# Down weight sums added by DMA, the last up tile and the first Down units in one order, own PSUM banks for the chains, another order of the gate stage

## The chip, the cores and the metric

The kernel runs on one core of a Trainium2 chip. The metric is the time of one execution on the device in microseconds. The kernel before took 2066.22 us (median of three runs, 2062.82 to 2066.92).

## The reference

One layer of a streaming encoder on 1056 tokens (1024 of a prompt, 32 of a sample; width 1024), all in float32:

```
z = rms(x) @ w_in            -> GLA q,k,v,r,gate | band q,k,v | merge gates gA,gB
mix = (sigmoid(gA)*(oa @ w_br_a) + sigmoid(gB)*(ob @ w_br_b)) @ w_out;   x += rms(mix)
a, g = split(rms(x) @ w_up)  (2 x 2816 columns)
y = (gelu(conv3(g)) * a) @ w_down;                                       x += rms(y)
gate = sigmoid(rms(x) @ w_ple_gate);                                     x += rms(gate * (p @ w_ple))
```

`oa` is a gated linear recurrence over four heads, `ob` a softmax attention over a band of chunks. Outputs are y, the keys and values, the recurrence states and the convolution state.

## The kernel before

Tokens lie along the free dimension, features along the 128 partitions. Every product is made of three TensorE products of halves (high x high, high x low, low x high), so each weight tile and each operand is split: ScalarE (ACT) copies to a rounded high part (`whi`, `mh`, `u`), VectorE (DVE) subtracts to get the low part (`wlo`, `ml`). SP issues the loads, POOL (GpSimd) issues most stores and the loads of Down's operands; each of these engines works through its own instructions in order.

The stages follow one another: w_in (52 projections, `project`, with the recurrence and the attention between), w_br_b, w_br_a, w_out, four up tiles as plain products (`up_plain`, `up_one`), 18 up tiles f = 4 to 21 by a Strassen-like scheme with seven products of quarter size (`up_strassen`, 24 matmuls of 264 columns each), Down (`down_unit`) and the gate stage.

The Strassen products read sums t1 to t4 of quarters of the normalised x, made from pairs of loads into the two `hn` buffers (`quarter_sums`, `quarter_third`, `quarter_last`); t4 is written over a part of `mh`/`ml` that the plain tiles read. `activate` (L1050) finishes an up tile: convolution, gelu, product, store to DRAM (`d_b`). After each odd tile `sums` makes four sums of the tile pair's rows, in `hn` buffers, one behind each product of the tiles that follow, and stores them too.

Down is such a scheme again: seven products q by four output pairs j, 28 units of 66 matmuls. Its row operands ("entries", two rows of 128 each) are loaded from `d_b` into `uraw` and split into nine `u` tiles; its weights are four sums of w_down's tiles, `d_s`, made in SBUF during w_br_a (`weight_sums`: 24 loads, 48 DVE operations, 24 stores). `chain(j)` gives a unit its PSUM banks: three sets "two" in turn, and "aux" for j = 3, which the sums of the norms (`sum_mm`) use too. `at(u, ...)` puts the norm's steps behind unit u: r1 (norm of the first half of y), `n_join` (residual added), r2 (norm for the gate), `n_oper` (operands); `MID` puts the norm's sums inside a unit. `presplit` splits w_ple_gate into `d_g` in units 2 to 16.

The gate stage goes through 24 tiles (8 "one" of 48 matmuls, then 16 of 24); `on(g, ...)` puts work behind tile g: `g_sig1` and `g_pair` (sigmoid), `g_mult` (product, square, sum of squares), the norm f1 of the first half, f3, and `final`, which adds into y by an accumulating DMA.

PE, DVE and ACT follow the written order in w_br_b to the plain up tiles and from Down on (`manual_schedule`); elsewhere a scheduler orders them by its own estimate. SP and POOL are ordered by the scheduler throughout.

## Time and profile before

| | |
|---|---|
| three runs | 2062.82, 2066.22, 2066.92 us |
| profiled execution | 2066.53 us, span 2064.5 us, mean granted TensorE clock 0.972 |
| TensorE, VectorE, ScalarE, GpSimd busy | 95%, 62%, 46%, 21% of the span |

A window of the trace gives, for each engine, the time it was busy and its instructions; the clock is the share of full speed granted to TensorE. A line of the waits reads: engine, tile and line that waited, what released it, microseconds in total, times, and the longest. In a timeline a row has its start, its duration, engine, line, operation, out<-in, and in brackets the idle time ahead of it and what ended that. Places in the trace, in microseconds of the span: w_in up to 900, w_br_b and w_br_a to 1070, w_out to 1170, plain up tiles to 1280, Strassen up tiles to 1680, Down to 1932, gate stage to the end.

### The profile page before, as it was taken

How to read it: one execution, taken by the hardware profiler on the slowest of the kernel's cores; microseconds unless marked ns; L12 is line 12 of the kernel's file. 1: busy time of each engine (PE TensorE's matmuls, PEld its weight loads, DVE VectorE, ACT ScalarE, POOL GpSimd, SP SyncE). 2: the span in 40 equal slices, each digit the busy share in tenths (PEclk: the TensorE clock that was granted, in tenths of full speed). 3: DMA queues.
4: the chain of work that ended last, by engine and by line, in shares of the span. 5: the costliest groups of instructions: out<-in, count | busy, mean ns of one | idle time of the engine just before them, and what ended most of it. 6: DMA issues, size and time to landing. Idle time of an engine off the chain costs nothing. (4 is left out here: it accounts for less than half of the span.)

```text
span 2064.5 us, 34547 instructions
## 1 busy us (share of the span) xinstructions
PE 1953.1 (95%) x13584; PEld 1908.2 (92%) x13584; DVE 1288.8 (62%) x2538; ACT 941.6 (46%) x1691; POOL 426.6 (21%) x489
## 2 busy tenths in 40 slices
PE   8999999999999999989998999799999979997985
PEld 7999999999999999989997999699999979997985
DVE  7556655465465663765763776677777764566565
ACT  6455556364553744643223554243334344454444
POOL 4422322321121211112320111011111121124102
PEclk9999999999999999999999999899999979998997
DMA  7212212211321212277984455523222358875667
GB/s 271 65 54 81 70 45 75 61 63 53 98 73 60 91 53 93 78 218 251 358 303 142 145 169 187 172 89 120 89 94 89 110 179 292 294 240 192 195 202 151
DMA packets 107534, 292.30 MB, mean 142 GB/s; under 512 B 12260, under 2 KB 36780, under 8 KB 107372
## 3 DMA queue, kind: packets, MB, share of 16 engines
q1 hardware_dynamic: 85420, 218.12, 32.0%
q0 software_dynamic: 21664, 71.63, 10.3%
q8 instruction: 106, 1.74, 0.3%
q14 instruction: 56, 0.46, 0.1%
q10 hardware_dynamic: 288, 0.36, 0.1%
HBM read 200.21 MB, written 89.85 MB: 141 GB/s over the span
## 5 line engine op out<-in xcount | busy, mean ns | idle before, releaser
L225 PE MATMUL mm<-xh,whi 128*128 128x352 f32 x1248 | 412.0, 330 | 0.0
L227 PE MATMUL mm<-xh,wlo 128*128 128x352 f32 x1248 | 411.8, 330 | 0.0
L226 PE MATMUL mm<-xl,whi 128*128 128x352 f32 x1248 | 409.7, 328 | 0.0
L205 POOL TENSOR_TENSOR wlo<-raw,whi 128x512 fp32r<-128x512 f32 x130 | 181.4, 1399 | 719.4 <-ACT whi L204 666.8
L225 PEld LDWEIGHTS mm<-xh,whi 128*128 128x128 f32 x1248 | 235.3, 189 | 1.6 <-DVE ev L349 0.4
L226 PEld LDWEIGHTS mm<-xl,whi 128*128 128x128 f32 x1248 | 235.0, 188 | 1.7 <-issue 0.3
L227 PEld LDWEIGHTS mm<-xh,wlo 128*128 128x128 f32 x1248 | 234.6, 188 | 1.1
L1395 PE MATMUL two<-u,whi 128*128 128x264 f32 x984 | 189.1, 292 | 6.8 <-DVE u L1360 3.8
L1214 PE MATMUL two<-mh,whi 128*128 128x264 f32 x576 | 164.0, 289 | 13.2 <-ACT mh L1151 8.0
L1215 PE MATMUL two<-ml,whi 128*128 128x264 f32 x576 | 165.2, 288 | 3.1 <-DVE ml L1152 3.1
L1395 PEld LDWEIGHTS two<-u,whi 128*128 128x128 f32 x984 | 158.8, 196 | 8.4 <-DVE u L1360 4.6
L1216 PE MATMUL two<-mh,wlo 128*128 128x264 f32 x576 | 164.9, 287 | 0.0
L204 ACT ACTIVATE whi<-raw 128x512 fp32r<-128x512 f32 (+1 forms) x146 | 89.6, 621 | 162.6 <-PE mm L226 99.2
L1395 PE MATMUL two<-u,wlo 128*128 128x264 f32 x492 | 143.5, 292 | 2.0 <-DMA wlo<-d_g 2.0
L1214 PEld LDWEIGHTS two<-mh,whi 128*128 128x128 f32 x576 | 109.2, 191 | 14.9 <-ACT mh L1151 8.9
L1215 PEld LDWEIGHTS two<-ml,whi 128*128 128x128 f32 x576 | 110.3, 191 | 3.9 <-DVE ml L1152 3.9
L1216 PEld LDWEIGHTS two<-mh,wlo 128*128 128x128 f32 x576 | 110.3, 192 | 0.0
L1395 PEld LDWEIGHTS two<-u,wlo 128*128 128x128 f32 x492 | 96.5, 196 | 2.4 <-DMA wlo<-d_g 2.4
L349 DVE TENSOR_TENSOR ev<-mm,rstd 128x352 f32<-128x352 f32 x120 | 61.4, 518 | 55.6 <-PE mm L227 55.0
L1204 ACT ACTIVATE whi<-ws 128x512 fp32r<-128x512 f32 x72 | 45.5, 632 | 103.2 <-PE two L1215 76.9
L1395 PE MATMUL two<-u,dhi 128*128 128x264 f32 x452 | 86.1, 291 | 2.0 <-ACT dhi L1386 2.0
L225 PE MATMUL mm<-mh,ahi 128*128 128x352 f32 x240 | 78.8, 328 | 8.9 <-ACT ahi L880 8.9
(490 smaller groups left out, 5147.8 us busy)
## 6 DMA issues: line engine op xcount, KB each, us to landing
raw<-in_w_in SPq DMA_DIRECT2D x52, 512.0 KB, 3.8
uraw<-d_b POOLq DMA_DIRECT2D x38, 528.0 KB, 5.8
raw<-in_w_up SPq DMA_DIRECT2D x27, 512.0 KB, 3.6
hn<-d_hn SPq DMA_DIRECT2D x24, 528.0 KB, 4.5
draw<-d_s SPq DMA_DIRECT2D x16, 704.0 KB, 4.6
d_b<-hn POOLq DMA_DIRECT2D x20, 528.0 KB, 4.7
d_b<-av POOLq DMA_DIRECT2D x33, 264.0 KB, 2.4
sraw<-in_w_up SPq DMA_DIRECT2D x17, 512.0 KB, 4.0
```

The source lines that it names most:

```text
L204: ac.activation(hi[-1][:, d], raw[:, b], AF.Copy)
L205: eng.tensor_tensor(lo[-1][:, d], raw[:, b], hi[-1][:, d], op=ALU.subtract)
L225: pe.matmul(ps, h, xh(kt), start=(first and i == 0), stop=False)
L226: pe.matmul(ps, h, xl(kt), start=False, stop=False)
L227: pe.matmul(ps, l, xh(kt), start=False, stop=(last and i == n - 1))
L349: return lambda ps, s: ve.tensor_tensor(t[:, s], ps, rstd(s), op=ALU.mult)
L1204: ac.activation(h, x, AF.Copy)
L1214: pe.matmul(ps[:, j, :HC], w[0][:, k], x[0][:, k, s], start=st, stop=False, skip_group_check=True)
L1215: pe.matmul(ps[:, j, :HC], w[0][:, k], x[1][:, k, s], start=False, stop=False, skip_group_check=True)
L1216: pe.matmul(ps[:, j, :HC], w[1][:, k], x[0][:, k, s], start=False, stop=sp_, skip_group_check=True)
L1395: pe.matmul(ps, w, x, start=st, stop=sp_, skip_group_check=True)
```

## The change

Seven edits that hang together:

1. **Down weight sums.** `d_s` is made during w_in by `down_sums`: 16 plain copies from DRAM to DRAM on SP and 16 accumulating DMAs on POOL, one DMA of 704 KB at each of the first 32 projections. Signs are chosen so that only additions are needed; `evac` and the row sums take the other signs.
2. **presplit** goes from Down into the w_br_a loop, on that loop's `ev` tiles.
3. **Order around the plain up tiles.** `quarter_third` comes ahead of the activation of tiles 1 and 2, and no row sums stand ahead of it.
4. **Row sums** no longer use the tiles in SBUF: `activate` stores both halves of each tile, and `row_sums` reads four rows back, makes the four sums and stores each. ROW_JOBS hangs the pairs on tiles 5, 6, 7, 9, 11 and so on; the last pair's go behind units 1 and 2.
5. **Last up tile and first units.** Tile 21 is written in one fixed order with the first four entries' loads (in `hn` buffers) and splits and unit 0's weights (`ahead`); its last quarter is finished behind the splits of entries 4 and 5. Entries live in the rows of `mh`/`ml` (`slots`) and one more tile.
6. **PSUM and norms in Down.** The chains have four named sets; the sum for r1 stands at the start of unit 21, that for r2 in unit 25, and the steps around them are moved; a unit's weights are split ahead of the evacuation of the unit before.
7. **Gate stage.** The sigmoid stands apart from the product (`g_sig`), a square is added when the next comes (`settle`), the products of the first half stand earlier, f1's total at tile 13, and all of f3's `final` behind the last tile.

```diff
+    def down_sums():
+        def step(d, src, j):
+            if src[0] == "sum":
+                x = d_s[src[1], j]
+            else:
+                x = wd[2 * j + src[1], :, src[2]]
+            if d in have:
+                tc.keep_in_program_order(po.dma_start(d_s[d, j], x, accum_op=ALU.add))
+            else:
+                tc.keep_in_program_order(dma.dma_start(d_s[d, j], x))
...
     def project(n, evac):
+        next(sums_left, None)
...
-        for i in range(2 if n in (1, 2, 3, 4) else 1):
-            weight_sums(*parts.pop(0))
-    cp.release()
+        presplit(n)
...
+    def row_sums(i, tile):
+        x, y = tile(), tile()
+        for t, k, d in ((x, 0, B12), (x, 1, B11), (y, 0, B22), (y, 1, B21)):
+            po.dma_start(t[:, k], d[i])
+        yield
+        for o, p, q, op, d in (...):
+            ve.tensor_tensor(o, p, q, op=op)
+            po.dma_start(d[i], o)
+            yield
...
+            if f in ROW_JOBS and muls[0] > 2:
+                next(ROW_JOBS[f], None)
...
-    activate(1, *open_[1, 0])
-    sum_rows(4)
     for f in range(3, UP_PLAIN):
         open_[f, 0] = up_one(f)
     quarter_third()
-    activate(2, *open_[2, 0])
+    for f in range(1, 3):
+        activate(f, *open_[f, 0])
     quarter_last()
...
+    def ahead(m):
+        if m == 3:
+            first_rows()
+        if m < 5:
+            split_entry(m - 3)
+            load_entry(m - 1, hn_tile)
+        elif m == 5:
+            split_entry(2)
+        else:
+            split_weights(0)
+            split_entry(3)
...
     def chain(j):
-        return tl(psum, [P, 2, 512], tag="two" if j < 3 else "aux", bufs=3 if j < 3 else 1)
+        return tl(psum, [P, 2, 512], tag=("c0", "c1", "c2", "aux")[j], bufs=1)
...
-    for i, u in enumerate((22, 22, 23, 23)):
+    for i, u in enumerate((21, 22, 22, 23)):
...
-    at(23, n_total, "r2", "a2")
-    at(24, n_inv, "r2")
+    at(24, n_total, "r2", "a2")
+    at(25, n_inv, "r2")
...
-    MID = {21: lambda: n_sum("r1"), 24: lambda: n_sum("r2")}
+    MID = {21: (0, lambda: n_sum("r1")), 25: (3, lambda: n_sum("r2"))}
...
+    split_entry(4)
+    load_entry(7)
+    split_entry(5)
+    load_entry(8)
+    last_up[2]()
     down_unit(0)
+    split_weights(1)
-    activate(FT - 1, *last_up)
+    activate(FT - 1, *last_up[:2])
...
+        settle(acc)
+        waiting[id(acc)] = i, sq
...
-    on(10, g_one, 0)
-    on(11, g_one, 1)
-    on(12, g_one, 2)
-    on(13, g_one, 3)
-    on(14, n_total, "f1", "g1")
+    on(5, g_one, 0)
+    on(7, g_one, 1)
+    on(11, g_one, 2)
+    on(12, g_one, 3)
+    on(13, n_total, "f1", "g1")
...
-    on(22, final, "f3", 0, three)
-    on(22, final, "f3", 1, three)
...
-    final("f3", 3, three)
+    for i in range(1, 4):
+        final("f3", i, three)
```

How the instructions move on VectorE, at three places. First, behind the last operand sums t1 and t2, while the last plain up tile runs (`gc`: convolution of an up tile, `av`: its product, `hn<-av`: row sums, `xs<-hn` and `t3l`: the operand t3). Before:

```order
L1061 TENSOR_TENSOR av_12365<-gc_12869,av_12365 128x32
L1076 TENSOR_TENSOR hn_12880<-av_12365,hn_12880 128x528
L1076 TENSOR_TENSOR hn_12881<-av_12365,av_12188 128x528
L1076 TENSOR_TENSOR hn_12881<-av_12365,hn_12880 128x528
L1055 SCALAR_TENSOR_TENSOR gc_13103<-gx_12520,vec_69,gc_13103 128x1058
L1205 TENSOR_TENSOR wlo_13182<-raw_13170,whi_13181 128x512
L1056 SCALAR_TENSOR_TENSOR gc_13103<-gx_12520,vec_69,gc_13103 128x1058
L1205 TENSOR_TENSOR wlo_13216<-ws_13212,whi_13215 128x512
L1060 TENSOR_TENSOR av_12521<-gc_13103,av_12521 128x1024
L1061 TENSOR_TENSOR av_12521<-gc_13103,av_12521 128x32
L1055 SCALAR_TENSOR_TENSOR gc_13153<-gx_12888,vec_69,gc_13153 128x1058
L1171 TENSOR_TENSOR xs_13075<-hn_13072,hn_13071 128x528
```

and now:

```order
L1074 SCALAR_TENSOR_TENSOR gc_12765<-gx_12152,vec_69,gc_12765 128x1058
L1075 SCALAR_TENSOR_TENSOR gc_12765<-gx_12152,vec_69,gc_12765 128x1058
L1176 TENSOR_TENSOR xs_13022<-hn_13019,hn_13018 128x528
L1079 TENSOR_TENSOR av_12153<-gc_12765,av_12153 128x1024
L1080 TENSOR_TENSOR av_12153<-gc_12765,av_12153 128x32
L1204 TENSOR_TENSOR ws_13167<-raw_13128 128x512
L1074 SCALAR_TENSOR_TENSOR gc_13050<-gx_12329,vec_69,gc_13050 128x1058
L1204 TENSOR_TENSOR ws_13169<-ws_13167,raw_13127 128x512
L1204 TENSOR_TENSOR ws_13260<-raw_13127,raw_13128 128x512
L1157 TENSOR_TENSOR t3l_13017<-xs_13022,t3h_13016 128x528
L1176 TENSOR_TENSOR xs_13030<-hn_13027,hn_13026 128x528
L1075 SCALAR_TENSOR_TENSOR gc_13050<-gx_12329,vec_69,gc_13050 128x1058
```

The row sums in the `hn` tiles are gone from here, and the first two pairs of t3 stand where the convolution of tile 1 stood.

Second, at the end of the last up tile (`c`, `av`, `gx`: its results, `two`: PSUM, `u<-uraw` before and `ml<-hn` now: the low part of an entry of Down, `wlo<-raw`: unit 0's or the tile's weights). Before:

```order
L1259 TENSOR_TENSOR av_17265<-av_17265,two_17396 128x528
L1387 TENSOR_TENSOR wlo_17529<-raw_17517,whi_17528 128x384
L1262 TENSOR_TENSOR c_2629_17269<-p_2628_17268,two_17395 128x528
L1263 TENSOR_TENSOR gx_17264<-gx_17264,c_2629_17269 128x528
L1232 TENSOR_TENSOR gx_17264<-c_2629_17269,two_17396 128x264
L1233 TENSOR_TENSOR gx_17264<-c_2629_17269,two_17396 128x232
L1234 TENSOR_TENSOR gx_17264<-c_2629_17269,two_17396 128x32
L1360 TENSOR_TENSOR u_17501<-uraw_17507,u_17501 128x2x528
L1360 TENSOR_TENSOR u_17536<-uraw_17509,u_17536 128x2x528
L1360 TENSOR_TENSOR u_17541<-uraw_17511,u_17541 128x2x528
```

and now:

```order
L1356 TENSOR_TENSOR ml_10331<-hn_17298,mh_10330 128x1056
L1212 TENSOR_TENSOR wlo_17451<-ws_17320,whi_17450 128x512
L1356 TENSOR_TENSOR ml_10331<-hn_17300,mh_10330 128x1056
L1204 TENSOR_TENSOR ws_17483<-raw_17302,sraw_17303 128x512
L1212 TENSOR_TENSOR wlo_17486<-ws_17483,whi_17485 128x512
L1267 TENSOR_TENSOR c_2624_17311<-p_2623_17310,two_17327 128x528
L1268 TENSOR_TENSOR av_17307<-av_17307,c_2624_17311 128x528
L1356 TENSOR_TENSOR ml_10331<-hn_17424,mh_10330 128x1056
L1271 TENSOR_TENSOR av_17307<-av_17307,two_17328 128x528
L1366 TENSOR_TENSOR wlo_17543<-raw_17418,whi_17542 128x512
L1366 TENSOR_TENSOR wlo_17547<-raw_17418,whi_17546 128x512
L1366 TENSOR_TENSOR wlo_17551<-raw_17419,whi_17550 128x384
```

The low parts of the entries stand among the tile's last products and results, where they stood behind all of them.

Third, in units 22 to 25 of Down (`z<-z,vec,rs` and `z<-z,pr`: join with the residual, `acc`: squares, `y`: operand of the norm's sum, `z<-z,aux`: evacuation of unit 23). Before:

```order
L1360 TENSOR_TENSOR u_19808<-uraw_19806,u_19808 128x528
L1493 SCALAR_TENSOR_TENSOR z_17648<-z_17648,vec_69,rs_19605 128x528 x2
L1498 TENSOR_TENSOR z_17648<-z_17648,pr_2949_19701 128x2x528
L1452 TENSOR_TENSOR acc_19707<-acc_19707,pr_19817 128x1056
L1493 SCALAR_TENSOR_TENSOR z_17648<-z_17648,vec_69,rs_19605 128x528 x2
L1498 TENSOR_TENSOR z_17648<-z_17648,pr_2965_19811 128x2x528
L1452 TENSOR_TENSOR acc_19707<-acc_19707,pr_19824 128x1056
L1456 TENSOR_TENSOR acc_19707<-acc_19707 128x528
L1459 TENSOR_TENSOR y_2969_19829<-acc_19707,y_2968_19828 128x528
L1435 TENSOR_TENSOR z_17648<-z_17648,aux_19716 128x528
L1437 TENSOR_TENSOR z_17648<-z_17648,aux_19716 128x528
```

and now:

```order
L1356 TENSOR_TENSOR ml_10331<-uraw_19665,mh_10330 128x528
L1541 SCALAR_TENSOR_TENSOR z_17692<-z_17692,vec_69,rs_19564 128x528 x2
L1546 TENSOR_TENSOR z_17692<-z_17692,pr_2896_19667 128x2x528
L1499 TENSOR_TENSOR acc_19579<-acc_19579,pr_19679 128x1056
L1474 TENSOR_TENSOR z_17692<-z_17692,aux_19682 128x528
L1476 TENSOR_TENSOR z_17692<-z_17692,aux_19682 128x528
L1499 TENSOR_TENSOR acc_19579<-acc_19579,pr_19774 128x1056
L1504 TENSOR_TENSOR acc_19579<-acc_19579 128x528
L1507 TENSOR_TENSOR y_2916_19862<-acc_19579,y_2915_19861 128x528
L1478 TENSOR_TENSOR z_17692<-z_17692,c_2859_19376 128x528
```

Two joins stood between the last entry and the operand `y`, now one; unit 23's evacuation stood behind `y` and stands ahead of the total.

372 lines of the change are left out of this document (191 added, 181 removed).

## The prediction

> **What bounds the kernel now.** I read the busy times on the page, then the waits of TensorE, then a table of 25 us windows around each dip, then the timelines of the engine that each wait names.
>
> ```profile
> PE 1953.1 (95%) x13584; PEld 1908.2 (92%) x13584; DVE 1288.8 (62%) x2538; ACT 941.6 (46%) x1691; POOL 426.6 (21%) x489
> ```
>
> TensorE is busy 95% of the span, no other engine over 62%. The change keeps every matmul of the program (as many per shape and per product on either side), so it can gain only what TensorE loses: time in which it waits, and time in which its clock is granted at less than full speed behind a wait. The windows give both (columns: busy us and count of PE, weight loads, DVE, ACT, POOL; granted clock; DMA share; GB/s):
>
> ```profile
> 975.00:1000.00 25.00, 21.94 (x121) 20.62 (x120) 18.46 (x31) 9.33 (x16) 5.56 (x6) 0.93 1.04 414
> 1075.00:1100.00 25.00, 15.42 (x92) 14.26 (x90) 8.87 (x15) 5.19 (x10) 2.90 (x4) 1.00 0.74 259
> 1100.00:1125.00 25.00, 22.31 (x125) 22.08 (x126) 7.52 (x11) 10.32 (x18) 0.00 (x0) 0.86 0.25 77
> 1275.00:1300.00 25.00, 21.77 (x163) 20.85 (x162) 15.41 (x23) 9.35 (x16) 1.61 (x4) 1.00 0.65 216
> 1300.00:1325.00 25.00, 13.90 (x95) 12.19 (x94) 20.00 (x34) 4.88 (x8) 2.62 (x4) 0.81 0.64 214
> 1325.00:1350.00 25.00, 22.35 (x153) 22.04 (x154) 15.46 (x23) 8.92 (x12) 1.71 (x6) 0.78 0.21 75
> 1500.00:1525.00 25.00, 25.00 (x208) 25.00 (x206) 18.05 (x30) 9.37 (x14) 4.58 (x10) 1.00 0.36 122
> 1675.00:1700.00 25.00, 15.46 (x71) 14.06 (x72) 15.10 (x18) 8.55 (x11) 8.95 (x12) 0.61 0.67 229
> 1700.00:1725.00 25.00, 25.00 (x192) 25.00 (x191) 12.39 (x16) 10.53 (x16) 3.63 (x5) 0.91 0.90 318
> 1875.00:1900.00 25.00, 13.96 (x116) 13.75 (x114) 20.09 (x21) 10.62 (x15) 9.11 (x8) 0.84 0.75 256
> 1900.00:1925.00 25.00, 24.60 (x182) 24.64 (x183) 11.88 (x15) 10.34 (x14) 9.93 (x9) 0.88 0.27 88
> 2000.00:2025.00 25.00, 15.79 (x107) 15.28 (x106) 16.45 (x21) 12.18 (x16) 1.38 (x2) 0.80 0.64 212
> 2025.00:2050.00 25.00, 20.34 (x145) 18.05 (x143) 14.86 (x29) 13.10 (x22) 7.31 (x7) 0.92 0.90 181
> ```
>
> The row at 1500 is the undisturbed case: 208 matmuls of 264 columns in 25 us, 0.120 us each. I count the loss of a window as 25 minus busy times clock (975: 25 - 21.94 x 0.93 = 4.6). That gives five holes:
> - around w_br_a and w_out (975, 1075, 1100): 4.6 + 9.6 + 5.8 = 20.0
> - first Strassen up tile (1275, 1300, 1325): 3.2 + 13.7 + 7.6 = 24.5
> - start of Down (1675, 1700): 15.6 + 2.3 = 17.9
> - second norm of Down (1875, 1900): 13.3 + 3.4 = 16.7
> - first norm of the gate stage and the last tiles (2000, 2025): 12.4 + 6.3 = 18.7
>
> Together 97.8 us. The waits name what four of them stand on:
>
> ```profile
> PE aux L1467 <- DVE z L1437: 11.4, 1, 11.4
> PE aux L1467 <- ACT y L1458: 9.1, 1, 9.1
> PE mm L225 <- ACT ahi L880: 8.9, 2, 7.6
> PE two L1214 <- ACT mh L1151: 8.0, 3, 4.2
> ```
>
> **The change, part by part.** *Down weight sums and w_ple_gate split.* 48 DVE sums, 24 loads and 12 pairs of stores leave the w_br_a loop; 16 plain copies on SP and 16 accumulating DMAs on POOL take their place, one in each of the first 32 of the 52 w_in projections, and the w_ple_gate split comes from Down into the loop (per iteration one 512 KB load, one ACT copy, one DVE subtraction, two stores). What the removed work did to w_out:
>
> ```profile
> 1081.37 0.33 SPq L875 DMA_DIRECT2D raw<-in_w_out  x1
> 1092.55 1.92 SPq L947 DMA_DIRECT2D res<-in_x  x4
> 1094.57 0.89 SPq L875 DMA_DIRECT2D raw<-in_w_out  x2
> ```
>
> SP issues one w_out load at 1081.4 and then sits to 1092.55 before the res loads, whose memory the sums' tiles had; the next w_out weights stand behind them; ACT's split of them (L880) is the 7.6 us wait. The last sums' loads also hold DVE, and the window at 975 has the DMA engines full (1.04). With these tiles gone res needs nothing but freed memory.  I take 13 of 20.0: the gate split's own load lands late in each iteration and the third w_out tile still waits for a free raw buffer. Bounds 6 and 18.
>
> In the w_in stage the cover is the lead of the loads:
>
> ```profile
> raw<-in_w_in SPq DMA_DIRECT2D x52, 512.0 KB, 3.8
> 121.57 0.33 SPq L195 DMA_DIRECT2D raw<-in_w_in  x1
> 133.90 0.63 ACT L204 ACTIVATE whi<-raw 128x512 fp32r<-128x512 f32 x1 [1.40 <-issue]
> ```
>
> 12.3 us from issue to use against 3.8 us to land, so 8 us spare, while one more 704 KB transfer per projection takes, at the 318 GB/s that the window at 1700 reached, 4.5 us for read and write together. On POOL an accumulate stands ahead of half of the low weight parts; it depends on a transfer four or more projections older. Taken +1, for two copies that stand ahead of x loads at the start; bounds 0 and +6.
>
> *First Strassen tile.*
>
> ```profile
> 1248.51 0.83 SPq L1190 DMA_DIRECT2D sraw<-in_w_up  x2
> 1270.85 8.21 SPq L1146 DMA_DIRECT2D hn<-d_hn  x4
> 1324.01 0.70 DVE L1152 TENSOR_TENSOR ml<-xs,mh 128x528 fp32r<-128x528 f32 x1
> ```
>
> Eight pairs of hn loads feed the operands t3 and t4, one pair at a time since there are two buffers. SP has none of them to issue from 1248.5 to 1270.85, because the row sums of the first pair of tiles hold both buffers until they are stored; then 53 us pass to the last split of t4 at 1324, which the seventh product waits for. Now the loads stand ahead of these sums: first pair at about 1249, the same 53 us later 1302, against a seventh product due at about 1282 + 6 x 2.9 = 1299 (24 matmuls of 0.120 us each). What is late next is row-sum work again: on DVE the first sum of tile 5 stands ahead of t4's last split, and waits for a load that can only start when that buffer is free; 5 us. So a stall of 3 + 5 us remains, plus some 2 us at the tile's start, where the window at 1275 loses 3.2: 24.5 - 10 = 14.5, taken 15; bounds 7 and 21.
>
> *Row sums read back from DRAM.* As many DVE sums as before (four per pair), but four loads and six single stores on POOL where two stores of two rows were. POOL gets 69 rows more in all.
>
> ```profile
> uraw<-d_b POOLq DMA_DIRECT2D x38, 528.0 KB, 5.8
> d_b<-av POOLq DMA_DIRECT2D x33, 264.0 KB, 2.4
> 1695.67 0.70 DVE L1076 TENSOR_TENSOR pr<-av 128x528 f32<-128x528 f32 x1
> 1695.95 0.57 POOL L1068 DMA_DIRECT2D d_b<-av  x1 [4.25 <-DVE av L1061]
> ```
>
> The loads are issued when a tile starts, the first sum comes after its third product, 8.7 us later; landing takes 2.4 to 5.8 us. DVE is in order, so a late load would hold the weight splits behind it, which have three products (8.7 us) of lead in four buffers. Taken +2 over ten tiles; bounds 0 and +12. The last two rows show a POOL issue of 0.57 us inside a DVE sum of 0.70 us: neither is held. The Trainium skill, "SBUF — State Buffer", section "SBUF: two separate sides", says that GpSimd cannot write the descriptors of its DMAs while a two-port DVE operation holds the shared port. Here the pair of rows speaks against it for these float32 sums; by the rule each added issue would wait out such a sum, 69 x 0.7 = 48 us of POOL time, nearly all of it behind the 8.7 us lead.
>
> *Last up tile and first units in one order.*
>
> ```profile
> 1682.72 1.08 ACT L1359 ACTIVATE u<-uraw 128x1056 fp32r<-128x1056 f32 x1 [9.31 <-DMA uraw<-d_b]
> 1683.83 1.26 DVE L1360 TENSOR_TENSOR u<-uraw,u 128x1056 fp32r<-128x1056 f32 x1 [5.60 <-ACT u L1359]
> ```
>
> Before, three entries are split when unit 0 starts and the fourth waits 9.3 us for a load that the freed buffer let go late. Now four entries go through hn buffers and into mh/ml rows during the tile. I followed the new order with 5.8 us per load, 1.08 + 1.26 us per split: unit 0 starts about 1 us late on its first weight part, entry 4 is 1 us late, and unit 1 finds its low weights 2 us late, because entry 5 and the deferred last quarter of the tile (five sums, 2.4 us) stand ahead of them on DVE. 4 to 5 remain of 17.9: taken 13; bounds 7 and 17.
>
> *Norm of Down.* The 11.4 us stand at unit 24, where the sum for r2 wants the aux bank that unit 23 filled:
>
> ```profile
> 1898.31 0.71 DVE L1459 TENSOR_TENSOR y<-acc,y 128x528 fp32r<-128x528 f32 x1 [0.71 <-ACT y L1458]
> 1899.55 0.70 DVE L1437 TENSOR_TENSOR z<-z,aux 128x528 f32<-128x528 f32 x1
> ```
>
> TensorE was there at 1888.8 (1900.2 less 11.4), the operand and the bank came at 1899.0 and 1900.2. The sum now stands one unit (66 x 0.120 = 7.95 us) later, at 1896.8; the joins stand up to one unit earlier, and the unit's evacuation ahead of the total and DVE no longer waits for the squares (below). 1900.2 less some 4 us of DVE work brought forward is 1896: 0 to 2 us of stall. The bank set by itself does not give this: the sums still share aux with the fourth unit. Behind it the four operands of the gate stage end some 2 us before they are needed. Taken 12 of 16.7; bounds 5 and 16.
>
> *Gate stage.*
>
> ```profile
> 1994.57 1.25 DVE L1690 TENSOR_TENSOR z<-uraw,draw 128x1056 f32<-128x1056 f32 x1
> 2007.56 1.26 DVE L1452 TENSOR_TENSOR acc<-acc,raw 128x1056 f32<-128x1056 f32 x1 [1.15 <-ACT raw L1448]
> 2015.76 0.71 DVE L1459 TENSOR_TENSOR y<-acc,y 128x528 fp32r<-128x528 f32 x1 [0.71 <-ACT y L1458]
> 2031.10 12.31 DMA wlo<-d_g
> ```
>
> Each product's square costs DVE a wait of 1.15 us for ACT; deferred, it costs none. From the first product at 1994.57 to the operand took 21 us. Two of the four products move ahead, two remain with two of the next group: five operations of 1.25, three of 0.7 and ACT's and DVE's last 1.4, some 10.5 us, so 2005, where TensorE is at 2015.8 - 9.1 = 2006.6. So that wait goes. The last row, from the chain of waits, is late next: the last gate weights, loaded beside the accumulating y stores, land at 2043.4 with TensorE behind them; without the slower clock (15.79 x 0.20 = 3.2 in the window at 2000) it reaches them some 3 us earlier against the same stores. Taken 9 of 18.7; bounds 3 and 14. The tail:
>
> ```profile
> out_y<-z POOLq DMA_DIRECT2D x6, 264.0 KB, 5.3
> ```
>
> That is issue to landing over the last 24 us. Two of the six stores move behind the last tile, into the queue ahead of the last two: +2; bounds 0 and +5, one such landing.
>
> Sum: -13 + 1 - 15 + 2 - 13 - 12 - 9 + 2 = -57 against the profiled execution's 2066.53 (span 2064.5 and 2.0 around it; the median of the three runs, 2066.22, is 0.3 below). 2066.5 - 57 = 2009.5; I say **2010 us**.
>
> Beside the small stalls that I leave: the Trainium skill, "TensorE: Matmul & The Clock Gate", Part 1, lets the clock halve only after an idle window of about 3.4 us. Here the window at 1325 has 0.78 behind waits of at most 4.2 us (L1151's row): not decided. By the rule stalls of 1 to 3 us would cost themselves alone; by the windows at 1300 and 1325 (13.8 us idle, 7.6 lost to the clock) half as much again, 8 us on the 15 that I leave, so 2018 in place of 2010.
>
> **Rivals.**
> - *The stalls move.* Each hole is several late things in line, and taking the last away leaves the next: entry 5 and the low weights in unit 1, t4's split behind a row sum, the operands of the gate stage with 2 us to spare, the gate weights. For: every one of these has under 3 us of slack. Against: DVE is at 62%, with 7 us free in each 25 us of the up stage. With half of each gain: -62/2 + 5 = -26, 2040 us.
> - *The row sums block DVE (slower).* In the ten up tiles with a job, sums wait in DVE's queue for loads that stand behind stores on POOL. Price: what the landing exceeds 8.7 us (to the third product) plus 8.7 us (the weight lead) stops TensorE. From 17.4 us on it loses; at 24 us each job costs 7 us and some clock, ten of them 90 us: 2066 - 57 + 75 or more, some 2090 us. For: each job's loads wait for the job before to store, in the two tiles that follow one another. Against: landings of 2.4 and 5.8 us at DMA shares of 0.36.
> - *The changed order does not free the hn loads*, so the Strassen hole stays and the start of Down with it: -57 + 28 = -29, near the first rival, 2038 us; little speaks for it, as the loads stand ahead of the sums in SP's queue.
> - *Everything closes.* All gains at their upper bounds but the clock's remainder: -86 + 5 gives 1985 us.
>
> **How the numbers follow.** Forecast (1990 to 2026) 0.62; stalls move or hn stays (2026 to 2060) 0.24; everything closes (below 1990) 0.06; within 0.2% (4 us, what a measurement here can tell from no change) 0.02; slower 0.06. So faster 0.92, same 0.02, slower 0.06. Range for 8 in 10: 1991 to 2042, from all terms near their upper bounds with the costs at theirs, to a little beyond half of the gains.
>
> **What would show it.** In the changed profile: SP's hn loads from about 1249 without the gap (shifted by what was gained before); no wait on L880's successor over 2 us; the norm sum at unit 25 under 2 us; a 25 us window at the start of Down with over 150 matmuls; a granted clock of 1.00 in the windows of the five holes; the up stage's windows still at 207 to 208 matmuls. Wrong would be windows of the up stage under 200 (the slower rival), or a new wait of TensorE over 5 us in w_in (the copies), in unit 1 (order of DVE) or at the last gate tiles.

## The result

The changed kernel takes **1993.51 us** (median of four runs, 1990.40 to 1996.98) against 2064.52 us for the kernel before (four runs, 2061.34 to 2066.92): a ratio of 0.9657, with a 95% interval of 0.9635 to 0.9680. The profiled execution took 1990.4 us, with a span of 1988.7 us against 2064.5, so 75.8 us less. The forecast was 2010 us: the sign and the mechanism held, and the gain was larger than the sum of the terms (57): 71.0 us by the medians and 75.8 by the two profiles. The profile of the changed kernel is of the fastest of its four runs and that of the kernel before lies 2 us above its median, so what is read from the pair below may overstate the gain by some 5 us.

The page of the changed kernel, busy times and granted clock in 40 slices:

```profile
PE 1925.1 (97%) x13584; PEld 1884.3 (95%) x13584; DVE 1258.3 (63%) x2490; ACT 938.2 (47%) x1691; POOL 456.9 (23%) x558
PEclk9999999999999999999999999999999999999998
```

The matmuls are the same in number, and TensorE is busy for 28 us less, which fits the matmuls that ran at a low clock behind the stalls: in the prediction's windows of the five holes busy time times the missing share of the clock comes to some 30 us. The clock row is now at 9 up to its last slice. VectorE has 48 instructions fewer, GpSimd 69 more, as the diff says.

The windows of the changed kernel around the five places (columns as in the prediction):

```profile
975.00:1000.00 25.00, 25.00 (x157) 25.00 (x156) 16.48 (x27) 10.90 (x20) 5.49 (x4) 1.00 0.88 313
1075.00:1100.00 25.00, 25.00 (x158) 25.00 (x157) 9.50 (x15) 11.43 (x21) 0.00 (x0) 1.00 0.36 116
1250.00:1275.00 25.00, 21.33 (x144) 21.04 (x143) 19.17 (x28) 9.65 (x15) 5.67 (x10) 0.93 0.70 230
1275.00:1300.00 25.00, 23.22 (x190) 22.84 (x189) 21.36 (x35) 8.95 (x14) 7.83 (x16) 1.00 0.58 201
1625.00:1650.00 25.00, 22.77 (x184) 22.29 (x183) 19.17 (x25) 11.78 (x17) 6.85 (x10) 1.00 0.75 257
1650.00:1675.00 25.00, 25.00 (x209) 25.00 (x208) 18.04 (x24) 15.45 (x23) 9.14 (x16) 1.00 0.82 299
1850.00:1875.00 25.00, 24.93 (x206) 24.73 (x205) 18.63 (x21) 9.85 (x11) 4.42 (x3) 1.00 0.52 168
1950.00:1975.00 25.00, 19.20 (x140) 17.31 (x138) 19.95 (x38) 15.98 (x27) 7.90 (x8) 0.91 0.89 196
```

The hole around w_out is gone altogether, those of Down are down to 2 us, and the first Strassen tile still loses some 7 us (1250 and 1275: 25 - 21.33 x 0.93 = 5.2, and 1.8). The last window holds the end of TensorE's work. Between 1300 and 1625 us the 25 us windows hold 207 or 208 matmuls, but for one with 203. The waits of TensorE in the changed kernel, those with the most time in all first:

```profile
PE mm L225 <- DVE ev L306: 6.1, 4, 2.2
PE mm L225 <- ACT bh L230: 5.0, 2, 3.7
PE aux L1882 <- DVE acc L1877: 3.7, 1, 3.7
PE two L1221 <- ACT av L1102: 3.7, 1, 3.7
```

No wait is over 3.7 us; before, the longest was 11.4. The first two, at the start of w_in and of w_br_b, were there before, at 4.3 us in three and 3.8 us in two.

**Where the 75.8 us came from.** Both traces hold 13584 matmuls, so I number them from the start and compare the start of the same number in both; the difference between two places is what the stage between them gained or lost. The places are chosen where both kernels have done the same work: the sum for r2, for one, stands in another unit now, and the norm's stage ends behind both.

| stage | predicted (bounds) | measured |
|---|---|---|
| start and w_in | +1 (0 to +6) | 0.0 |
| w_br_b to w_out | -13 (-18 to -6) | -20.9 |
| plain up tiles and first Strassen tile | -15 (-21 to -7) | +1.2 - 18.0 = -16.8 |
| Strassen tiles with row jobs | +2 (0 to +12) | +0.6 |
| start of Down | -13 (-17 to -7) | -18.3 |
| norm of Down | -12 (-16 to -5) | -11.0 |
| gate stage | -9 (-14 to -3) | +3.1 - 13.4 = -10.3 |
| behind the last matmul | +2 (0 to +5) | +0.9 |
| sum | -57 | -75.8 |

### The profile page after: what moved, and what is told of

It reads as the page before. It is cut to its first block, busy times and chain, and to the rows that moved or that the text cites. A ratio compares the mean times of both kernels' runs of the same rounds, so it can differ in the third digit from the quotient of the medians.

```text
span 1988.7 us, 34585 instructions
## 1 busy us (share of the span) xinstructions
PE 1925.1 (97%) x13584; PEld 1884.3 (95%) x13584; DVE 1258.3 (63%) x2490; ACT 938.2 (47%) x1691; POOL 456.9 (23%) x558
## 4 chain that ended last, share of the span: by engine, by line
PE 68%; DVE 14%; DMA 6%; ACT 6%; issue 5%; SPq 0%; POOL 0%; ACTq 0%; DVEq 0%; POOLq 0%
PE mm L225 11%; PE mm L226 11%; PE mm L227 11%; PE c L1436 7%; PE two L1221 5%; PE two L1222 5%; PE two L1223 5%; DMA hn<-d_hn 3%; PE aux L1436 2%; PE two L756 2%; PE one L534 2%; PE one L492 1%; DVE z L1541 1%; DVE d L724 1%; PE two L476 1%
## 5 line engine op out<-in xcount | busy, mean ns | idle before, releaser
L1436 PE MATMUL c<-ml,whi 128*128 128x264 f32 x438 | 124.2, 283 | 0.7 <-DVE ml L1356 0.7
L1436 PE MATMUL c<-mh,whi 128*128 128x264 f32 x438 | 124.5, 284 | 0.0
L1436 PE MATMUL c<-mh,wlo 128*128 128x264 f32 x438 | 124.3, 284 | 0.1
L1436 PEld LDWEIGHTS c<-ml,whi 128*128 128x128 f32 x438 | 82.5, 188 | 0.9 <-DVE ml L1356 0.9
L1436 PEld LDWEIGHTS c<-mh,wlo 128*128 128x128 f32 x438 | 82.2, 188 | 0.3 <-DMA wlo<-d_g 0.3
L1436 PEld LDWEIGHTS c<-mh,whi 128*128 128x128 f32 x438 | 82.5, 188 | 0.0
```

The costliest lines, as they stand in the source:

```text
L1436: pe.matmul(ps, w, x, start=st, stop=sp_, skip_group_check=True)
```

## The experiments

Each run takes the changed kernel and alters one thing. "Place" in a result is the same comparison by matmul number, now against the changed kernel's profile. What two profiles of one order of work differ by at such a place can be read from the run with the earlier row sums, below: 2.3 us at w_br_b, 3.7 over the first Strassen tile as a whole, and under 1 us from the first units of Down on.

### The Down weight sums and the split put back

```diff
-        next(sums_left, None)
...
-        presplit(n)
+        for i in range(2 if n in (1, 2, 3, 4) else 1):
+            weight_sums(*parts.pop(0))
+    cp.release()
...
+    for n in range(KT):
+        at(2 + 2 * n, presplit, n)
```

The first line is in `project`, the next in the w_br_a loop, the last in Down; `weight_sums` and `presplit` themselves are those of the kernel before.

> The changed kernel with its first two edits undone: the Down weight sums are made again in SBUF inside the w_br_a loop (24 loads, 48 DVE sums, 24 stores) and w_ple_gate is split again in Down. Theory (the tiles of these sums hold memory and the SP and DVE queues into w_out): the 21 us that the profiled executions differ by around w_br_a and w_out come back, 2008 to 2016 us, and the w_in stage stays as it is within 1 us. Rival (that gain came from the order of other work around it): within 5 us of the changed kernel, 1990 to 1998.

Measured: 2007.06 us, ratio to the kernel before 0.9733 (0.9712 to 0.9755), span +17.7. It loses 6.0 by the first oa loads, 14.1 around w_br_a and w_out and 1.9 at the start of Down, and gains 1.5 in w_in and 2.0 behind the last matmul. The time is just under the range that was expected. SP's timeline, then SP's waits between 1040 and 1120 us and TensorE's between 1060 and 1120 us, of this run:

```profile
1077.15 0.33 SPq L910 DMA_DIRECT2D raw<-in_w_out  x1
1090.12 1.92 SPq L982 DMA_DIRECT2D res<-in_x  x4
...
SPq L872 <- DMA d_s<-half: 16.8, 7, 6.3
SPq L982 <- DMA d_s<-half: 12.5, 1, 12.5
...
PE mm L227 <- DVE alo L916: 4.5, 1, 4.5
PE mm L225 <- ACT ahi L915: 4.4, 1, 4.4
```

The gap that the prediction quoted is back, and the wait names it: the res loads stand 12.5 us for the stores of the last sums, and the w_out weights behind them, for whose two parts TensorE then waits 4.5 and 4.4 us, with half the clock behind each. In the changed kernel the same timeline reads:

```profile
1066.04 1.87 SPq L966 DMA_DIRECT2D res<-in_x  x3
1069.85 0.34 SPq L894 DMA_DIRECT2D raw<-in_w_out  x1
...
1072.67 9.27 SPq L894 DMA_DIRECT2D raw<-in_w_out  x4
```

### Only the split of w_ple_gate put back to Down

```diff
-        presplit(n)
...
+    for n in range(KT):
+        at(2 + 2 * n, presplit, n)
```

> The changed kernel with only the split of w_ple_gate put back into Down. Theory (the Down sums alone made the hole around w_br_a and w_out): that region stays as in the changed kernel within 1 us, and Down, which has room on ACT and DVE, loses 0 to 3 us: 1990 to 1997. Rival (the load of the split on DVE and ACT in Down is a part of what went at the start of Down and at its norm): 5 to 12 us more there.

Measured: 1990.36 us in one run, span +0.0; 0.9 less by the end of w_br_b, -3.2 and +2.7 around the first Strassen tile, which the edit does not touch, +1.8 at the start of Down. The split costs nothing that shows in the w_br_a loop, so the previous run's loss there belongs to the weight sums. At the start of Down TensorE waits 2.2 us in all, as in the changed kernel, but in three short waits and with 3.4 us at half clock behind them, which makes up the 1.8; the other two runs with the split in Down lose 1.9 and 2.0 there, so some 2 us may be its price in that place.

### The old sums, but finished earlier

```diff
-        for i in range(2 if n in (1, 2, 3, 4) else 1):
+        for i in range(2 if n < 6 else 0):
             weight_sums(*parts.pop(0))
```

The edit is shown against the run with the sums put back, the measurements against the changed kernel.

> Against the run in which the weight sums and the split of w_ple_gate were put back as before (span 2006.4 us, +17.7 against the changed kernel: 6.0 by the first oa loads and 14.1 around w_br_a and w_out), one edit: all twelve parts of the sums stand in the first six of the eight iterations of w_br_a, where that run has two in iterations 1 to 4 and one in the others. The work stays the same. Theory (the res loads and the first w_out loads stand in SP's queue behind the last sums, whose tiles hold the memory of res): with two iterations between the last sum and w_out the hole at w_out falls from 14 us to under 4, SP's gap before the res loads closes, and the loss at the oa loads stays or grows by a few us, since the loads crowd earlier. Rival (it is the amount of transfers and VectorE work in this loop, wherever it stands): the loss only moves ahead, and w_br_a and w_out together still lose 14 us or more against the changed kernel.

Measured: 2003.18 us in one run, span +12.8; 5.1 at the oa loads, 10.1 around w_out. So the hole at w_out shrank from 14.1 to 10.1, where the theory wanted under 4: it fails. The rival asked for 14 or more over w_br_a and w_out: with the oa loads, which are the first of w_br_a, it is 15.2 and the rival holds; counted without them, as the 14.1 was, it does not. SP's waits between 1040 and 1120 us of this run say why:

```profile
SPq L872 <- DMA d_s<-half: 19.8, 6, 6.6
SPq L982 <- DMA d_s<-half: 9.5, 1, 9.5
```

Written into iteration 5, the last sums still ran at 1081 to 1083 us, because the chain of load, sum and store through four buffers is slower than the loop: it waits 19.8 us for its own stores. The res loads stand behind the same stores as before, 9.5 us in place of 12.5. So most of the cost stays wherever the parts are written (12.8 of 17.7 us): it is that chain, with the memory that it holds.

### Row sums of the first pair ahead of the third tile again

```diff
-    ROW_JOBS = {...: row_sums(i, hn_tile) for i in range(FH - 1)}
+    ROW_JOBS = {...: row_sums(i, hn_tile) for i in range(1, FH - 1)}
+    activate(1, *open_[1, 0])
+    for i in row_sums(0, hn_tile):
+        pass
     for f in range(3, UP_PLAIN):
         open_[f, 0] = up_one(f)
     quarter_third()
-    for f in range(1, 3):
-        activate(f, *open_[f, 0])
+    activate(2, *open_[2, 0])
```

> The changed kernel with the convolution of tile 1 and the first pair's row sums put ahead of the loads for t3, in the hn buffers, as before. Theory (the row sums hold both hn buffers, so the loads for t3 and t4 start late): the first hn load of t3 goes out 12 to 22 us later, and the first Strassen tile loses 12 to 17 us more: 2004 to 2011. Rival (what was gained there came from fewer stores and loads beside it): under 5 us.

Measured: 2012.75 us, ratio 0.9765 (0.9745 to 0.9784), span +20.6, with +19.3 over the first Strassen tile: 4.3 are saved at its start, where the wait for the last plain tile (L1102) is 0.9 us and not 3.7, and 23.6 lost behind that. This is more than the 12 to 17 us expected. SP's timeline of this run and TensorE's longest wait in it:

```profile
1228.60 1.04 SPq L1197 DMA_DIRECT2D sraw<-in_w_up  x2
1255.97 2.06 SPq L1151 DMA_DIRECT2D hn<-d_hn  x2
...
PE two L1221 <- ACT mh L1156: 11.9, 3, 5.3
```

From 1229.6 SP issues nothing for 26 us, and the first hn load of t3 goes out 14.4 us later than in the changed kernel; the wait for the high part of t4 is back. In the changed kernel the loads go on where the gap was (SP, then VectorE):

```profile
1241.57 23.06 SPq L1151 DMA_DIRECT2D hn<-d_hn  x9
...
1285.86 0.70 DVE L1092 TENSOR_TENSOR hn<-hn 128x528 f32<-128x528 f32 x1
1286.48 0.70 DVE L1157 TENSOR_TENSOR ml<-xs,mh 128x528 fp32r<-128x528 f32 x1
```

The last split of t4 ends at 1287; before it ended at 1325, less the 20 us gained by then 1305. It is 18 us earlier, which is what the place gained. The row sum ahead of it (L1092) runs without a wait.

### The first entries split behind the last product

```diff
-        if m < 5:
-            split_entry(m - 3)
-            load_entry(m - 1, hn_tile)
-        elif m == 5:
-            split_entry(2)
-        else:
-            split_weights(0)
-            split_entry(3)
+        if m < 6:
+            return
+        split_weights(0)
+        for e in range(4):
+            split_entry(e)
+            if e < 2:
+                load_entry(e + 2, hn_tile)
```

> The changed kernel with the splits of the first four entries of Down and their loads 2 and 3 put behind the last product of the last up tile, still in one fixed order and in the same buffers. Theory (the splits among the products fill the hole at the start of Down): 10 to 18 us come back there, 2003 to 2011. Rival (the earlier load of unit 1's weights and the deferred last quarter did it): under 6 us.

Measured: 1998.07 us, ratio 0.9687 (0.9666 to 0.9709), span +9.0, of which +7.5 at the start of Down; less than expected. TensorE's waits between 1630 and 1690 us of this run:

```profile
PE c L1435 <- ACT mh L1355: 2.2, 1, 2.2
PE c L1435 <- DVE ml L1356: 2.2, 3, 0.9
PE c L1435 <- DVE dlo L1366: 1.6, 1, 1.6
```

The loss comes as five waits of up to 2.2 us on the splits, not as one stall. They come to 6.0 us against 2.2 in the changed kernel (the last, for unit 1's low weights, is there too, with 1.5), and behind them the clock was at half for 6.8 us, which costs the other half of the loss. Unit 0 reads its entries one after another, so each split needs to be only just ahead of it.

### The old names of the PSUM sets

```diff
-        return tl(psum, [P, 2, 512], tag=("c0", "c1", "c2", "aux")[j], bufs=1)
+        return tl(psum, [P, 2, 512], tag="two" if j < 3 else "aux", bufs=3 if j < 3 else 1)
```

> The changed kernel with the PSUM names of before: three sets in turn and aux. Theory (the norm sums share aux with the fourth chain in both, so the names do nothing): the same order of instructions, within 1 us at every stage, 1990 to 1997. Rival (the set for the norm sums is what lets the sum for r2 through): 5 to 12 us more at units 24 and 25.

Measured: 2002.12 us in one run, span +11.7. At the sums of the norms nothing changed (0.0). But the start of Down lost 10.7, which nothing of mine had foreseen. TensorE's longest wait in this run:

```profile
PE two L1436 <- DVE gx L1243: 11.5, 1, 11.5
```

L1243 is the last sum of `last_quarter`, the piece of the last up tile that the change puts behind the splits of entries 4 and 5. It reads a PSUM bank, and the first unit of Down wanted that same bank.

### The four sets made in another order

```diff
-    places = [chain(j) for j in (3, 2, 0, 1)]
+    places = [chain(j) for j in (0, 1, 2, 3)]
```

> Against the changed kernel (span 1988.7 us), one edit: the four PSUM sets of Down are made in the order 0, 1, 2, 3, where the changed kernel makes them in the order 3, 2, 0, 1; the four names stay distinct. Only which physical bank a unit gets is other. Theory (from the run with the old names, which lost 10.7 us at unit 0 with a wait of 11.5 us for the last up tile's deferred quarter): what counts is which bank unit 0 and unit 1 get at the start of Down. With the order 0, 1, 2, 3 the set of unit 0 comes first and so lies elsewhere than in the changed kernel; if it lies over the last up tile's still unread results, TensorE stops some 10 us at unit 0 or, where unit 1's set lies there, less than 4 us at unit 1. All other stages stay within 2 us. Rival (the names, that is four sets of one buffer against three shared buffers, made the difference, and not the place): no loss at the start of Down, span within 2 us of the changed kernel.

Measured: 1999.76 us, ratio 0.9707 (0.9693 to 0.9722), span +6.1; +8.7 at the start of Down, and at no other place more than 2.3. The names are distinct and every engine runs the same instructions in the same order as in the changed kernel; only the banks are others. TensorE's timeline of this run:

```profile
1642.24 0.56 PE L1436 MATMUL c<-mh,whi 128*128 128x264 f32 x1 [9.61 <-DVE c L1276]
```

Unit 0 now waits 9.6 us for L1276, the first instruction of the same deferred piece, which reads the tile's other late bank. So it is the bank that counts: the deferred reads cost nothing where the next user of their bank comes later still. In the changed kernel unit 0 has another bank and begins at 1635.2, right behind the last up product, with no wait:

```profile
1635.25 0.29 PE L1436 MATMUL c<-mh,whi 128*128 128x264 f32 x1
```

### The norm for the gate one unit earlier

```diff
-    at(24, n_total, "r2", "a2")
-    at(25, n_inv, "r2")
-    for i, u in enumerate((26, 26, 26, 27)):
+    at(23, n_total, "r2", "a2")
+    at(24, n_inv, "r2")
+    for i, u in enumerate((25, 26, 26, 27)):
...
-    MID = {21: (0, lambda: n_sum("r1")), 25: (3, lambda: n_sum("r2"))}
+    MID = {21: (0, lambda: n_sum("r1")), 24: (3, lambda: n_sum("r2"))}
```

> The changed kernel with the total, the sum and the inverse for r2 one unit earlier, as before (total behind unit 23, sum inside unit 24). Theory (one unit more is what gives the operand and the bank their time): TensorE waits 5 to 10 us at that sum, 1999 to 2005. Rival (earlier joins and the deferred squares already bring the operand in time): under 3 us.

Measured: 1998.87 us, ratio 0.9707 (0.9691 to 0.9724), span +8.4: +1.4 ahead of r2, which is no more than two profiles differ by, +8.4 at r2, and 1.6 given back behind it. TensorE's longest wait in this run:

```profile
PE aux L1515 <- DVE z L1476: 9.8, 1, 9.8
```

It is the wait of the kernel before (11.4 on z), on the same bank, and it comes back with the four own names in force.

### Squares added at once

```diff
         ac.activation(sq, src, AF.Square)
-        settle(acc)
         waiting[id(acc)] = i, sq
+        settle(acc)
```

> The changed kernel with each square added as soon as it is made. Theory: DVE waits some 1.1 us for ACT at each of about 20 squares again; the norms of Down and of the gate stage come 1 to 5 us later each: 2 to 8 us more in all, 1994 to 2003. Rival (the order alone did it): within 1 us.

Measured: 1998.62 us in one run, span +8.2. Of it 2.3 lie at r2, 0.5 between r2 and f1, 3.9 at f1 and 0.4 behind it; 4.1 more came at w_br_b and w_out, where the edit changes nothing, and 3.3 went again at the first Strassen tile. So deferring is worth some 7 us, most of it at f1 and r2. TensorE's waits from 1830 us on:

```profile
PE aux L1515 <- ACT y L1506: 4.7, 5, 1.7
```

Five short waits for the sums' operand against three (2.4 us) in the changed kernel: VectorE stands 16.6 us in all for ACT's squares at these additions, and 0.3 in the changed kernel.

### Products and f1 at their old places

```diff
-    on(5, g_one, 0)
-    on(7, g_one, 1)
-    on(11, g_one, 2)
-    on(12, g_one, 3)
-    on(13, n_total, "f1", "g1")
+    on(10, g_one, 0)
+    on(11, g_one, 1)
+    on(12, g_one, 2)
+    on(13, g_one, 3)
+    on(14, n_total, "f1", "g1")
...
-    on(10, g_sig, "g3", 3)
-    on(11, g_sig, "g3", 2)
+    on(11, g_sig, "g3", 3)
+    on(12, g_sig, "g3", 2)
...
```

The edit moves the loads of these products and the sigmoids of the next group back as well.

> The changed kernel with the gate stage's products of the first half, f1's total and its loads at the tiles of before; squares still deferred. Theory (two products moved ahead of the late norms are what brings f1's operand in time): TensorE waits 3 to 8 us at the sum for f1, 1994 to 2001. Rival (the deferred squares alone suffice): under 2 us.

Measured: 1997.32 us in one run, span +6.9: -1.8 before the gate stage, where the edit changes nothing, -1.5 in the gate stage ahead of f1, +7.4 around f1, +2.3 behind it. TensorE's longest wait from 1925 us on:

```profile
PE c L1436 <- ACT draw L1740: 4.9, 1, 4.9
```

The loss is not at the sum for f1, where the theory had it, but just ahead of it, at a sigmoid on ACT that holds a PSUM set (4.9 us, 1.2 in the changed kernel). The operand of f1 ended at 1947.4, 0.4 us after TensorE was ready for it; TensorE came that late because of the sigmoid, so the run does not show that the deferred squares alone would bring the operand in time. Nor does it part the places of the products from those of the sigmoids, which moved with them. The early products do cost something where they now stand: 1.5 of the 3.1 us that the changed kernel lost ahead of f1 come back.

### Row sums two products earlier

```diff
-            if f in ROW_JOBS and muls[0] > 2:
+            if f in ROW_JOBS and muls[0] > 0:
```

> Against the changed kernel (span 1988.7 us), one edit: in the ten Strassen up tiles with a row job, the first of the four sums stands behind the tile's first product and no longer behind its third, so 2.9 us and not 8.7 us lie between the loads' issue and the first sum on VectorE. The prediction's slower rival said that such a sum, waiting for its load, holds the weight splits behind it. Theory: the loads land 2.4 to 5.8 us after issue and the splits have three products (8.7 us) of lead in four buffers, so even a sum that waits some 3 us holds nothing that TensorE needs: 0 to +2 us in all, at most +1 us at any one tile. Rival (the lead is what hides the loads; VectorE's queue has no slack): each of the ten jobs costs 2 us or more, +20 us or more, with waits of TensorE for low weight parts (wlo) in tiles 5, 6, 7, 9, 11 and so on.

Measured: 1989.91 us, ratio 0.9673 (0.9652 to 0.9694), span -1.2. It tells the theories apart in nothing: the trace shows every matmul and every instruction of VectorE, ACT and GpSimd in the very order of the changed kernel. The scheduler had placed the sums by its own estimate, and the place where they are written had no part in it. The run is a second profile of the same order of work, and shows how far two such profiles differ: +2.3 at w_br_b, -1.4 and -2.3 at the first Strassen tile, 0.8 at most in the norms of Down and in the gate stage, 1.2 at the end. The rival that row sums block VectorE was thus not tested by an edit; what the trace of the changed kernel says of it stands below.

### The transfers of w_in done twice

```diff
                 tc.keep_in_program_order(po.dma_start(d_s[d, j], x, accum_op=ALU.add))
+                tc.keep_in_program_order(po.dma_start(d_t[d, j], x, accum_op=ALU.add))
             else:
                 tc.keep_in_program_order(dma.dma_start(d_s[d, j], x))
+                tc.keep_in_program_order(dma.dma_start(d_t[d, j], x))
```

Nothing reads `d_t`.

> Against the changed kernel (span 1988.7 us), one edit: each of the 16 copies and 16 accumulating transfers of 704 KB in the w_in stage is done twice, the second time into a tensor that nothing reads, so the first 32 projections carry 1.4 MB each beside their weights. The prediction put the single transfers at +1 us (0 to +6), hidden by some 8 us of lead that the weight loads have; the trace of the changed kernel shows 0.0 us by the end of w_in, with the DMA engines' mean busy share at 0.33 to 0.40 there where it was 0.20 before. Theory (there is room: the transfers use idle DMA time and nothing waits for them): the share rises to some 0.5 to 0.55, the weight loads land later but inside their lead, and the loss by the end of w_in stays under 4 us, most of it in the first 100 us, where the share is 0.61 already. Rival (the lead was about used up by the single transfers: 4.5 us each by the prediction's estimate, so 9 us for two against 8 us spare): each of the 32 projections loses about 1 us or more, 30 us or more in all, with waits of TensorE for whi or wlo of the w_in weights. Later stages stay as they are.

Measured: 1996.45 us, ratio 0.9703 (0.9686 to 0.9719), span +4.0; +5.6 by the end of w_in (2.1 in the first 64 us, 6.1 between 381 and 564 us, 2.6 of that given back by 655). A window of 100 us, of this run:

```profile
400.00:500.00 100.00, 97.18 (x637) 96.05 (x636) 62.32 (x189) 49.85 (x112) 30.00 (x37) 1.00 0.58 165
```

and of the changed kernel:

```profile
400.00:500.00 100.00, 99.59 (x659) 98.61 (x658) 63.72 (x197) 50.07 (x113) 25.85 (x33) 1.00 0.40 119
```

The rival (30 us or more) falls. The theory's figure (under 4) was a little low, and the loss lies not at the start, as it said, but mostly between 381 and 564 us; 2.4 us of it are one wait for a tile of the recurrence on ACT, and how the transfers delay that is not shown. One set of transfers is free; the second set begins to cost.

## Why the prediction was right, and where it was not

**What bounds the kernel, and the five holes.** Right. The five places gave 81.6 us (20.9, 18.0, 18.3, 11.0, 13.4), and all others together took 5.8 of it back. Of the signs that the prediction named, two came only in part: the clock was at 0.93 in the first Strassen tile and at 0.91 in the last tiles, not at 1.00, and one window of the up stage had 203 matmuls.

**Weight sums (-13 predicted, -20.9 measured, beyond the bound of 18).** The mechanism was right: with the sums put back SP stands 12.5 us before the res loads for the stores of the sums' tiles. What failed is the 7 us that I left: "the gate split's own load lands late in each iteration and the third w_out tile still waits for a free raw buffer". Neither costs TensorE anything. The split moved back alone changes the span by 0.0 us, and in the changed kernel SP does wait at the w_out loads (the row of 9.27 us for four), but at 1072 to 1082, in good time: the window at 1075 is full. I had priced a late load as a stall without asking whether it was still early for TensorE.

**The transfers in w_in (+1, measured 0.0).** Right, with the cover as given: the w_in weight loads land in 3.8 us in the median, as before. The estimate of 4.5 us for a transfer was low. Its landing times in the changed kernel:

```profile
d_s<-in_w_down POOLq DMA_DIRECT2D x16, 704.0 KB, 8.1
d_s<-in_w_down SPq DMA_DIRECT2D x8, 704.0 KB, 7.6
d_s<-d_s SPq DMA_DIRECT2D x8, 704.0 KB, 5.8
```

8 us each did not matter, since nothing waits for them and a projection takes longer than that. With twice the transfers the loss was 5.6 us.

**First Strassen tile (-15, measured -16.8).** Right in mechanism and nearly in size. The first hn pair went at 1241.6, the last split of t4 ended at 1287.2, 46 us behind it and not 53. The row sum that I put in front of that split for 5 us did stand there, but did not wait. What is left is 3.7 us at the tile's start on the evacuation of the last plain tile (L1102), with 1.7 us of clock behind it, in the place where I had left 2, and 1.8 us at 1295.4 on ACT's copy `p` (L1283). Of the 8 us that I left for the seventh product none came.

**Row sums read back (+2, measured +0.6).** Right in size, not in its reason. "The loads are issued when a tile starts" is wrong, as one job in the changed kernel shows (GpSimd, then VectorE):

```profile
1387.14 0.54 POOL L1088 DMA_DIRECT2D hn<-d_b  x1 [3.59 <-DMA d_b<-av]
1390.09 0.71 DVE L1092 TENSOR_TENSOR hn<-hn 128x528 f32<-128x528 f32 x1 [5.22 <-DMA hn<-d_b]
```

A job reads what the tile just finished has stored, so its load waits on GpSimd until that store has landed, and VectorE then waits for the load. Over the ten jobs these waits come to 59 us of VectorE (the idle column of two groups, the last but one number):

```profile
L1092 DVE TENSOR_TENSOR hn<-hn,hn 128x528 f32<-128x528 f32 x20 | 14.1, 707 | 26.3 <-DMA hn<-d_b 26.1
L1092 DVE TENSOR_TENSOR hn<-hn 128x528 f32<-128x528 f32 x20 | 14.1, 706 | 33.2 <-DMA hn<-d_b 33.2
```

That is the state from which the slower rival starts, and it still costs TensorE nothing: 59 us over ten jobs is 6 us each, under the 8.7 us of weight lead that the prediction set against it. The first part of the rival's margin, the 8.7 us from issue to the first sum, was not there; the second held. Where its threshold lies no run shows, since no job came near it. The loads themselves land as foreseen (issues between 1300 and 1620 us):

```profile
hn<-d_b POOLq DMA_DIRECT2D x32, 264.0 KB, 3.7
d_b<-hn POOLq DMA_DIRECT2D x36, 264.0 KB, 2.4
```

**The rule on GpSimd's descriptors.** By the rule of the Trainium skill ("SBUF — State Buffer", "SBUF: two separate sides"), as the prediction weighed it, the added issues would wait out float32 sums of VectorE. The trace goes on speaking against that for these sums: an issue takes 0.54 or 0.55 us (0.57 before), and where it waits it is for a store or for a sum to be done. One at 1410.5 runs beside two VectorE operations of 0.70 and 0.68 us and takes 0.55 us. The section "Who interferes with whom" of that page of the Trainium skill says of such sums that they have no two-port mode; there the trace agrees.

**Start of Down (-13, measured -18.3, beyond the bound of 17).** Two steps failed. The hole was drawn too small: it began one window earlier than I counted, as this row of the kernel before shows, with 2.2 us more:

```profile
1650.00:1675.00 25.00, 22.79 (x186) 22.41 (x184) 14.45 (x23) 11.60 (x16) 3.02 (x5) 1.00 0.32 106
```

And of the 4 to 5 us that I left, unit 0's late first weight part did not come; unit 1's low weights did, with 1.5 us. VectorE at that place in the changed kernel:

```profile
1640.76 2.56 DVE L1356 TENSOR_TENSOR ml<-uraw,mh 128x1056 fp32r<-128x1056 f32 x2 [3.29 <-ACT mh L1355]
...
1645.32 0.18 DVE L1243 TENSOR_TENSOR gx<-c,two 128x32 f32<-128x32 f32 x1
1645.42 1.76 DVE L1366 TENSOR_TENSOR dlo<-draw,dhi 128x512 fp32r<-128x512 f32 x3
```

The order is the one that I followed: entries 4 and 5, the deferred quarter, then unit 1's low weights (`dlo`). What I never asked is in which banks that piece waits. They are read up to 1645.5, when unit 0 has been running for ten microseconds; with one of them under unit 0, as in two of the runs, this costs 8.7 to 10.7 us, about half of the gain. The prediction reckoned on none of this, so that the changed kernel gave unit 0 another bank was, as far as the prediction goes, luck.

**Norm of Down (-12, measured -11.0).** Right in mechanism and nearly in size: the sum for r2 waits 0.9 us, where 0 to 2 were foreseen. One unit earlier it waits 9.8 us on the same bank, 8.4 net; the names alone give nothing there (0.0), as the prediction said. That they give nothing at all was not said but was taken for granted, and is wrong by the 10.7 us above.

**Gate stage (-9, measured -10.3).** The net is near because two errors go against each other. f1 and the last tiles gave 13.4, more than I took: the wait of 9.1 went, and so did the waits for the last gate weights. But 3.1 us were lost ahead of f1, which I had not foreseen. TensorE's waits in the changed kernel from 1830 to 1969 us (the first line has 0.6 us at r2's sum, 1.3 at r4's and 0.5 at r5's):

```profile
PE aux L1515 <- ACT y L1506: 2.4, 3, 1.3
PE c L1436 <- ACT draw L1740: 1.2, 1, 1.2
```

The wait at r4's sum stays with the products at their old places and is gone with r2 one unit earlier, so it goes with the later r2. The wait at r5's sum is gone with the old places (there and just behind it 1.5 us come back); the one for the sigmoid is longer there. So the earlier products cost half of the 3.1 us at most.

**Behind the last matmul (+2, measured +0.9).** Right.

**The clock.** The weighing of "TensorE: Matmul & The Clock Gate", Part 1, of the Trainium skill comes out for neither side as it was put. A wait well under 3.4 us can halve the clock: in the changed kernel the wait of 2.2 us that ended at 33.5 (L306) has 3.4 us at half clock behind it, as this window shows,

```profile
35.00:38.50 3.50, 2.92 (x11) 2.47 (x9) 3.40 (x3) 0.27 (x1) 2.10 (x1) 0.51 0.42 169
```

and so have three waits of 0.7 to 0.8 us in 3.6 us at the start of Down in the run with only the split put back. But it need not: 1.8 us at 1295.4 and 1.5 us at 1646.2 in the changed kernel left it at 1.00. So the idle window of about 3.4 us that this page of the Trainium skill puts ahead of the halved clock is not the shortest wait that costs clock; the measurement decides, and what tells the two cases apart is not shown here. The 8 us that the prediction set aside did not come, but not for the rule's sake: in the five holes few waits are left, and one of them, 3.7 us at the first Strassen tile, brings 3.4 us at half clock. The 15 us of stalls to which it applied the half are not what its terms leave, either: of 97.8 us they take 62.

**The rivals.** "Everything closes", with 1985 us, lies nearer to the measured 1993.5 than the forecast's 2010 does, though the time is still in the forecast's own range: two of the gains passed their upper bounds, and no other did. "The stalls move" fell: what was late next (entry 5 and unit 1's low weights, the operands of the gate stage) cost TensorE 1.5 us at most in any one wait, and t4's split none. "The row sums block DVE" fell with the 0.6 us above; no run made the sums later, so how near it was is not shown. "The changed order does not free the hn loads" is excluded by SP's timeline.

**In one sentence:** of the 18.8 us by which the sum fell short in the profiled pair, 7.9 are the weight sums, where I charged for lateness that no matmul met, and 5.3 the start of Down, where 2.2 were a hole drawn too small and the rest lateness that came to under half of what I charged.

## What to carry to other kernels

When a hole has a known cause, price what remains by asking of each late thing whether TensorE would have been there; a queue that waits is not yet a stall, and here a third of a gain was struck off for one that cost nothing. When an evacuation is put off, look for the next user of its PSUM bank: which physical bank that is, not the name, decided here between nothing and some 10 us. Find where a hole begins by windows on both sides of it before bounding a gain by its size.

## What the runs showed of the hardware that I had not expected

- An accumulating transfer from DRAM to DRAM of 704 KB lands in 8.1 us in the median, a plain copy of the same tensor in 7.6. 32 of them beside 52 weight loads of 512 KB cost TensorE 0.0 us, 64 of them 5.6.
- Two profiles of one order of instructions differ by up to 3.7 us over one stage, of either sign, while their ends agree within 1.2 us; the four timed runs of the changed kernel spread over 6.6 us.
- VectorE stood 59 us in total for loads in ten up tiles (and was busy for 63% of the span), and the stage lost 0.6 us.
- Three waits of TensorE of 0.7 to 0.8 us within 3.6 us were followed by 3.4 us at half clock in one run; single waits of 1.5 and 1.8 us in another were not.
